# Differential attention on one core: scores in one two-bank tile, projections in three single banks, and three steps moved to VectorE

## The chip, the cores and the metric

The kernel runs on one core of a Trainium2 chip. The metric is the device time of one execution in microseconds. TensorE is called PE in the profile, VectorE DVE, ScalarE ACT, GpSimd POOL and SyncE SP.

## The reference, cut to what matters

The program is a two-layer diffusion block: 512 latent tokens and 256 context tokens of width 1024. Layer 0 is a feed-forward block, windowed attention and a second feed-forward block; layer 1 has a feed-forward block, differential attention, a feed-forward block and the last norm. The change is in differential attention alone. It has 8 heads; each has two pairs of queries and keys of 64 elements and one value of 128, and only the 512 latent tokens ask:

```python
def diff_probs(s):
    p = jax.nn.softmax(s * scale, axis=-1)          # scale = 64 ** -0.5 = 0.125
    return p[:, :, 0] - lam * p[:, :, 1]

def head_out(o):
    o = _rmsnorm(o, subln_w) * (1.0 - lambda_init)
    return o.reshape(o.shape[0], o.shape[1], H * 2 * HD) @ w_out

s_lat = jnp.einsum('bqhjd,bkhjd->bhjqk', qb, kx)
s_ctx = jnp.einsum('bqhjd,bchjd->bhjqc', qb, kc)
p = diff_probs(jnp.concatenate([s_lat, s_ctx], axis=-1))
```

All of it is in float32. The kernel splits each operand of a matmul into a rounded high part and the rest (names in `h` and `l`), and multiplies high by high, high by low and low by high; the scores hold the high and low part of the 64 key rows stacked as 128 rows, and so take two matmuls.

## The kernel before, in words

A tile scheduler sets the order of the instructions of each engine, from the program's order, the buffers of each pool and its own costs. Each engine then works its list in order.

`diff` (L586 on) opens four pools of PSUM, which has eight banks of 512 columns: `pss` with four banks for scores (tile name `s`), `ptr` with two for transposes (`tr`), `pav` with one for the head's output (`av`) and `pbig` with one for projections (`half`). The loop runs over heads `h` 0 to 7. In each head `probs` is called for four blocks of 128 queries (0 to 3, called q0 to q3 here); after q1, q2 and q3 the next head's keys, queries and values are projected (`keys`, `queries`, `vals`); last comes `values` for the head. In the last head the place of the projections is taken by `out_proj(0, ...)`, which multiplies heads 0 to 3 with the output weights, and behind the loop by `out_proj(1, ...)` for heads 4 to 7. The first three projections, for head 0, use the score banks.

A projection (`project_halves`, L265) takes 24 matmuls into one bank, then 24 into another; `scaled_halves` (L288, DVE) reads each bank out, times the tokens' norm. `rope` rotates keys and queries: a bias (L310, ACT), a shuffle (L313, DVE), times the cosine (L314, POOL), times the sine (L315, here on POOL), and the sum (L318, DVE). `vals` transposes the values (L661), rounds them (`vh`, L663, ACT) and takes the rest (`vl`, L664, DVE).

`probs` works for each of the two pairs j = 0, 1 in two chunks of 384 keys. For each chunk there are two matmuls into an own bank (L678, L679) and a maximum over the chunk (L680, DVE). L683 joins the two maxima, and ACT takes two exponentials with their sums (L686). Then the sums are added (L690), inverted (L691) and the second is multiplied by lambda (L692), all on DVE; POOL scales the second pair's 768 columns (L694) and DVE makes the difference (L695).

`values` takes six blocks of keys: four transposes (L703), a rounding (`pth`, L706, ACT), the rest (`ptl`, L707, DVE) and three matmuls into `av` (L708 to L710). Then the head's norm: squares (L715, ACT), a sum over partitions by a matmul with ones, in two passes (L717, PE, into a `tr` bank), three ACT steps (L718 to L720), four steps on POOL (L721 to L724), the product (L725, DVE), the output's high part (L727, ACT) and low part (L728, DVE).

Of the kernel before, what the change touches and what calls it, by code (L numbers as in the profile page):

```python
# [10 lines left out]
F32 = mybir.dt.float32  # L11
# [6 lines left out]
P = 128  # L18
# [16 lines left out]
class Net:  # L35
# [229 lines left out]
    def project_halves(self, src, xonly=False, pool=None, tag="half"):  # L265

        w = self.weights(src)
        pool = pool or self.pbig
        mm = self.nc.tensor.matmul
        cuts = ((CTX, 512), (512, T + 2)) if xonly else ((0, 384), (384, T + 2))  # L270
        out = []
        for s, e in cuts:
            ps = pool.tile([P, 512], F32, name=tag)
            for k in range(ND):
                for i, (w_, x) in enumerate(((w[0], self.xh), (w[0], self.xl), (w[1], self.xh))):
                    mm(ps[:, :e - s], w_[:, k], x[:, k, s:e], start=(k == 0 and i == 0), stop=(k == ND - 1 and i == 2))  # L276
            out.append(ps)
        n = 256 if xonly else 384
        bias = self.sp.tile([P, 2], F32, name="bias")
        self.nc.vector.tensor_copy(out=bias, in_=out[1][:, n:n + 2])  # L280
        return out, bias

    def scaled_halves(self, ps, tag, xonly=False):
        u = self.tp.tile([P, T], F32, name=tag)
        s, n = (CTX, 256) if xonly else (0, 384)
        for i in range(2):
            tk = slice(s + i * n, s + i * n + n)
            self.nc.vector.tensor_tensor(out=u[:, tk], in0=ps[i][:, :n], in1=self.rstd[:, tk], op=ALU.mult)  # L288
        return u
# [296 lines left out]
    def diff(self, after):  # L586
        nc, a = self.nc, self.a
        pss = self.ps("pdiff_s", 4)
        ptr = self.ps("pdiff_t", 2)
        pav = self.ps("pdiff_v", 1)  # L590
        self.pbig = self.ps("pdiff", 1)
# [20 lines left out]
        early = self.project_halves(a["diff_in"][8], pool=pss, tag="s")  # L612
        self.norm_halves(pss)
# [7 lines left out]
        def keys(h, early=None):  # L621
# [3 lines left out]
            self.rope(u, bias, u[:, XT], nc.gpsimd)  # L625
# [25 lines left out]
        def vals(h, pool=None):  # L651
            ps, bias = self.project_halves(a["diff_in"][16 + h], pool=pool, tag="s" if pool else "half")
# [15 lines left out]
        def probs(ks, qs, qb):  # L668
            st = self.sp.tile([P, 12], F32, name="st4")
            out = []  # L670
            qc = slice(qb * P, (qb + 1) * P)
            for j in range(2):
                p = (pp, p1p)[j].tile([P, T], F32, name=f"p{j}")
                ss = []
                for c in range(2):
                    s = pss.tile([P, 512], F32, name="s")[:, :384]
                    kc = ks[j][:, c * 384:(c + 1) * 384]
                    nc.tensor.matmul(s, qs[j][0][:, qc], kc, start=True, stop=False)  # L678
                    nc.tensor.matmul(s, qs[j][1][:, qc], kc, start=False, stop=True)  # L679
                    nc.vector.tensor_reduce(out=st[:, 2 * j + c:2 * j + c + 1], in_=s, op=ALU.max, axis=AX.X)  # L680
                    ss.append(s)
                nm = st[:, 4 + j:5 + j]
                nc.vector.tensor_scalar(out=nm, in0=st[:, 2 * j:2 * j + 1], scalar1=st[:, 2 * j + 1:2 * j + 2],  # L683
                                        scalar2=-0.125, op0=ALU.max, op1=ALU.mult)
                for c in range(2):
                    nc.scalar.activation(out=p[:, c * 384:(c + 1) * 384], in_=ss[c], func=AF.Exp, bias=nm, scale=0.125,  # L686
                                         accum_out=st[:, 6 + 2 * c + j:7 + 2 * c + j])
                out.append(p)
            r = self.sp.tile([P, 2], F32, name="rr")
            nc.vector.tensor_tensor(out=r, in0=st[:, 6:8], in1=st[:, 8:10], op=ALU.add)  # L690
            nc.vector.reciprocal(out=r, in_=r)  # L691
            nc.vector.tensor_tensor(out=r[:, 1:2], in0=r[:, 1:2], in1=lam[:, 2:3], op=ALU.mult)  # L692
            p0, p1 = out
            nc.gpsimd.tensor_scalar(out=p1, in0=p1, scalar1=r[:, 1:2], scalar2=1.0, op0=ALU.mult, op1=ALU.mult)  # L694
            nc.vector.scalar_tensor_tensor(out=p0, in0=p0, scalar=r[:, 0:1], in1=p1, op0=ALU.mult, op1=ALU.add)  # L695
            return p0

        def values(h, ps_, vh, vl):
# [22 lines left out]
            nc.gpsimd.tensor_tensor(out=v, in0=v, in1=r0, op=ALU.mult)  # L721
            nc.gpsimd.tensor_tensor(out=v, in0=v, in1=r0, op=ALU.mult)
            nc.gpsimd.tensor_scalar(out=v, in0=v, scalar1=-0.5, scalar2=1.5, op0=ALU.mult, op1=ALU.add)
            nc.gpsimd.tensor_tensor(out=r0, in0=v, in1=r0, op=ALU.mult)  # L724
# [29 lines left out]
        ks, qs, vv = keys(0, early), queries(0, pss), vals(0, pss)  # L754
# [21 lines left out]
        self.pbig.release(); pav.release(); ptr.release(); pss.release()  # L776
# [353 lines left out]
```

## Time and profile before

| | us |
|---|---|
| median of 3 runs | 2852.33 |
| lowest, highest | 2849.23, 2855.4 |
| profiled execution: its time | 2853.44 |
| profiled execution: its span | 2851.6 |

The mean granted clock of TensorE in the profiled execution is 0.991. The span is the time from the first to the last instruction in the trace, and starts at 0 there. Differential attention lies between 2065.7, where its first projection starts, and 2439.7, where the first matmul starts that needs the last head's output: 374.0 us. In the profile a line such as `L288` is a line of the kernel; `out<-in` are the program's tile names; behind `|` stand busy time, mean duration of one in ns, and the idle time of the engine ahead of it with what ended it. A row of the windows gives, behind its length, the busy time and count of PE, PEld (TensorE's weight loads), DVE, ACT and POOL, then the granted clock, the DMA share and GB/s.

### The profile page before, as it was taken

The numbers are of one execution on the slowest core, as the hardware profiler recorded it, in microseconds if no ns is written. First come the engines' busy times: TensorE is split into PE (matmuls) and PEld (weight loads), VectorE is DVE, ScalarE is ACT, GpSimd is POOL, SyncE is SP. The second block draws the span as 40 slices with busy tenths as digits, with TensorE's granted clock in tenths as the row PEclk, the third lists the DMA queues.
The fourth block names the chain that finished last, engine by engine and source line by source line (L and its number), as shares of the span: only waits on it lengthen the run. The fifth ranks groups of instructions, "written<-read, shape, count | busy, mean of one in ns | idle before, by whom it ended". The sixth has DMA issues, their size and how long they took to land. (4 is left out here: it accounts for less than half of the span.)

```text
span 2851.6 us, 40866 instructions
## 1 busy us (share of the span) xinstructions
PE 2759.4 (97%) x16162; PEld 2578.0 (90%) x16162; DVE 1525.4 (53%) x2661; ACT 962.6 (34%) x1733; POOL 1279.3 (45%) x756
## 2 busy tenths in 40 slices
PE   6999999999899999999999999999999999899998
PEld 4999999989777999999999999999988887799998
DVE  8645455567887844444557333333567777422223
ACT  3212112245666422121233221221345655422223
POOL 1434333365433533333444434333555665555553
PEclk9999999999999999999999999999999999999999
DMA  7332432342331223223323233233232233233331
GB/s 277 107 127 97 140 111 98 123 138 81 84 127 38 89 85 117 86 85 121 94 81 111 84 104 102 71 115 115 73 99 82 82 90 121 73 100 93 101 103 45
DMA packets 105119, 290.09 MB, mean 102 GB/s; under 512 B 12512, under 2 KB 22880, under 8 KB 104928
## 3 DMA queue, kind: packets, MB, share of 16 engines
q1 hardware_dynamic: 104496, 287.37, 31.3%
q8 instruction: 128, 2.10, 0.3%
q14 instruction: 63, 0.52, 0.1%
q10 hardware_dynamic: 432, 0.11, 0.0%
HBM read 257.28 MB, written 12.06 MB: 94 GB/s over the span
## 5 line engine op out<-in xcount | busy, mean ns | idle before, releaser
L56 POOL TENSOR_TENSOR w_lo<-w_raw,w_hi 128x1024 fp32r<-128x1024 f32 (+2 forms) x377 | 804.1, 2133 | 1089.8 <-ACT w_hi L55 1066.9
L55 ACT CAST w_hi<-w_raw 128x1024 fp32r<-128x1024 f32 (+2 forms) x377 | 337.5, 895 | 1112.4 <-PE big L70 398.2
L257 PE MATMUL big<-xh,w_hi 128*128 128x384 f32 (+3 forms) x2816 | 689.8, 326 | 6.5 <-DVE xh L174 3.2
L257 PE MATMUL big<-xh,w_lo 128*128 128x384 f32 (+3 forms) x2816 | 688.7, 326 | 0.6 <-POOL w_lo L56 0.5
L257 PE MATMUL big<-xl,w_hi 128*128 128x384 f32 (+3 forms) x2816 | 686.8, 325 | 0.9 <-DVE xl L185 0.9
L257 PEld LDWEIGHTS big<-xh,w_hi 128*128 128x128 f32 x2816 | 499.4, 190 | 10.0 <-DVE tb L210 3.7
L131 DVE SCALAR_TENSOR_TENSOR ada_junk<-w_raw,s_bc 128x1024 f32<-128x1024 f32 x224 | 337.4, 1506 | 305.9 <-DMA w_raw<-ada_w 303.7
L257 PEld LDWEIGHTS big<-xl,w_hi 128*128 128x128 f32 x2816 | 496.8, 190 | 1.1 <-DVE xl L185 1.1
L257 PEld LDWEIGHTS big<-xh,w_lo 128*128 128x128 f32 x2816 | 494.6, 189 | 1.6 <-POOL w_lo L56 1.6
L262 DVE COPY bias<-big 128x2 f32<-128x2 f32 x176 | 27.6, 157 | 597.0 <-PE big L257 596.9
L68 PE MATMUL big<-hh,w_hi 128*128 128x512 f32 (+1 forms) x1200 | 327.4, 344 | 0.0
L72 PE MATMUL big<-hh,w_lo 128*128 128x512 f32 (+1 forms) x1200 | 326.8, 344 | 0.0
L70 PE MATMUL big<-hl,w_hi 128*128 128x512 f32 (+1 forms) x1200 | 326.8, 343 | 0.0
L302 DVE SCALAR_TENSOR_TENSOR hT<-big,mod,hT 128x512 f32<-128x512 f32 (+1 forms) x288 | 167.9, 618 | 180.9 <-PE big L72 180.6
L70 PEld LDWEIGHTS big<-hl,w_hi 128*128 128x128 f32 x1200 | 225.6, 188 | 30.0
L72 PEld LDWEIGHTS big<-hh,w_lo 128*128 128x128 f32 x1200 | 224.7, 188 | 28.8
L68 PEld LDWEIGHTS big<-hh,w_hi 128*128 128x128 f32 x1200 | 224.8, 188 | 27.1
L991 POOL TENSOR_TENSOR hl<-tb,hh 128x768 fp32r<-128x768 f32 (+1 forms) x88 | 151.5, 1722 | 169.9 <-ACT hh L990 158.1
L986 DVE SCALAR_TENSOR_TENSOR tb<-tb,bias,ta 128x512 f32<-128x512 f32 (+1 forms) x154 | 179.6, 1199 | 8.3 <-DVE tb L295 0.5
L276 PE MATMUL half<-xh,w_hi 128*128 128x384 f32 (+3 forms) x464 | 155.4, 335 | 20.3 <-DVE ta L288 18.2
L990 ACT CAST hh<-tb 128x768 fp32r<-128x768 f32 (+1 forms) x88 | 68.7, 781 | 268.4 <-DVE tb L986 268.4
L276 PE MATMUL half<-xl,w_hi 128*128 128x384 f32 (+3 forms) x464 | 153.7, 331 | 0.0
(224 smaller groups left out, 3595.6 us busy)
## 6 DMA issues: line engine op xcount, KB each, us to landing
w_raw<-ffn_gu SPq DMA_DIRECT2D x176, 512.0 KB, 3.3
w_raw<-ada_w SPq DMA_DIRECT2D x128, 512.0 KB, 3.3
w_raw<-ffn_d SPq DMA_DIRECT2D x96, 256.0 KB, 2.7
w_raw<-ffn_d SPq DMA_DIRECT2D x64, 320.0 KB, 2.9
w_raw<-diff_in SPq DMA_DIRECT2D x24, 512.0 KB, 3.2
w_raw<-gqa_in SPq DMA_DIRECT2D x12, 512.0 KB, 3.5
ada_raw<-ada_w SPq DMA_DIRECT2D x8, 512.0 KB, 9.4
ada_rawk<-ada_k SPq DMA_DIRECT2D x8, 512.0 KB, 7.8
```

The lines of the kernel that those rows point to most:

```text
L55: nc.scalar.copy(out=hi[:, :cols], in_=raw[:, :cols])
L56: nc.gpsimd.tensor_tensor(out=lo[:, :cols], in0=raw[:, :cols], in1=hi[:, :cols].bitcast(F32), op=ALU.subtract)
L68: nc.tensor.matmul(o, wh, xh, start=(k == 0), stop=False)
L70: nc.tensor.matmul(o, wh, xl, start=False, stop=False)
L72: nc.tensor.matmul(o, wl, xh, start=False, stop=(k == n - 1))
L131: getattr(nc, engines[s]).scalar_tensor_tensor(out=junk, in0=raw, scalar=1.0, in1=self.sbc[:, s], op0=ALU.mult, op1=ALU.mult, accum_out=se ...
L257: mm(ps[:, c, :e - s], w[:, k], x[:, k, s:e], start=first, stop=last)
L276: mm(ps[:, :e - s], w_[:, k], x[:, k, s:e], start=(k == 0 and i == 0), stop=(k == ND - 1 and i == 2))
L302: self.nc.vector.scalar_tensor_tensor(out=h, in0=o, scalar=self.mv(l, s, c, d), in1=h, op0=ALU.mult, op1=ALU.add)
L986: nc.vector.scalar_tensor_tensor(out=u[:, tk], in0=u[:, tk], scalar=bu[:, s:s + 1], in1=g[:, tk], op0=ALU.add, op1=ALU.mult)
L990: nc.scalar.copy(out=hh[:, toks], in_=u[:, toks])
L991: nc.gpsimd.tensor_tensor(out=hl[:, toks], in0=u[:, toks], in1=hh[:, toks].bitcast(F32), op=ALU.subtract)
```

## The change

- **Banks.** The score pool holds one tile of two banks in place of four single banks, and the projections get three single banks in place of one.
- **Scores.** For each pair j the four matmuls go into the two banks of the one tile; one maximum (negated) runs over 768 columns, and one exponential with one sum. The factor 0.125 moves into the queries, where it is applied with the norm, so the joining step, the adding of the sums and the product with lambda go.
- **Second pair's scaling.** One DVE step with two scalars (the inverse and lambda) in place of the step on POOL.
- **Rope.** The product with the sine is on DVE in keys and queries.
- **Head norm.** Three DVE steps in place of four on POOL.
- **First projections.** Keys, queries and values of head 0 go through the projection banks; the norm over all tokens takes the score tile.

```diff
-        pss = self.ps("pdiff_s", 4)
+        pss = self.ps("pdiff_s", 1)
+        self.pbig = self.ps("pdiff", 3)
         ptr = self.ps("pdiff_t", 2)
         pav = self.ps("pdiff_v", 1)
-        self.pbig = self.ps("pdiff", 1)
...
-        early = self.project_halves(a["diff_in"][8], pool=pss, tag="s")
-        self.norm_halves(pss)
+        early = self.project_halves(a["diff_in"][8])
+        self.norm_banks(pss)
...
-            self.rope(u, bias, u[:, XT], nc.gpsimd)
+            self.rope(u, bias, u[:, XT])
...
             for j in range(2):
                 p = (pp, p1p)[j].tile([P, T], F32, name=f"p{j}")
-                ss = []
-                for c in range(2):
-                    s = pss.tile([P, 512], F32, name="s")[:, :384]
-                    kc = ks[j][:, c * 384:(c + 1) * 384]
-                    nc.tensor.matmul(s, qs[j][0][:, qc], kc, start=True, stop=False)
-                    nc.tensor.matmul(s, qs[j][1][:, qc], kc, start=False, stop=True)
-                    nc.vector.tensor_reduce(out=st[:, 2 * j + c:2 * j + c + 1], in_=s, op=ALU.max, axis=AX.X)
-                    ss.append(s)
-                nm = st[:, 4 + j:5 + j]
-                nc.vector.tensor_scalar(out=nm, in0=st[:, 2 * j:2 * j + 1], scalar1=st[:, 2 * j + 1:2 * j + 2],
-                                        scalar2=-0.125, op0=ALU.max, op1=ALU.mult)
-                for c in range(2):
-                    nc.scalar.activation(out=p[:, c * 384:(c + 1) * 384], in_=ss[c], func=AF.Exp, bias=nm, scale=0.125,
-                                         accum_out=st[:, 6 + 2 * c + j:7 + 2 * c + j])
+                s = pss.tile([P, 2, 512], F32, name="s")[:, :, :384]
+                for i in range(2):
+                    for c in range(2):
+                        nc.tensor.matmul(s[:, c], qs[j][i][:, qc], ks[j][:, c * 384:(c + 1) * 384], start=(i == 0),
+                                         stop=(i == 1))
+                nc.vector.tensor_reduce(out=nm[:, j:j + 1], in_=s, op=ALU.max, axis=AX.XY, negate=True)
+                nc.scalar.activation(out=p.rearrange("p (c n) -> p c n", c=2), in_=s, func=AF.Exp, bias=nm[:, j:j + 1],
+                                     accum_out=sm[:, j:j + 1])
                 out.append(p)
-            r = self.sp.tile([P, 2], F32, name="rr")
-            nc.vector.tensor_tensor(out=r, in0=st[:, 6:8], in1=st[:, 8:10], op=ALU.add)
-            nc.vector.reciprocal(out=r, in_=r)
-            nc.vector.tensor_tensor(out=r[:, 1:2], in0=r[:, 1:2], in1=lam[:, 2:3], op=ALU.mult)
+            nc.vector.reciprocal(out=r, in_=sm)
             p0, p1 = out
-            nc.gpsimd.tensor_scalar(out=p1, in0=p1, scalar1=r[:, 1:2], scalar2=1.0, op0=ALU.mult, op1=ALU.mult)
+            nc.vector.tensor_scalar(out=p1, in0=p1, scalar1=r[:, 1:2], scalar2=lam[:, 2:3], op0=ALU.mult, op1=ALU.mult)
             nc.vector.scalar_tensor_tensor(out=p0, in0=p0, scalar=r[:, 0:1], in1=p1, op0=ALU.mult, op1=ALU.add)
...
-            nc.gpsimd.tensor_tensor(out=v, in0=v, in1=r0, op=ALU.mult)
-            nc.gpsimd.tensor_tensor(out=v, in0=v, in1=r0, op=ALU.mult)
-            nc.gpsimd.tensor_scalar(out=v, in0=v, scalar1=-0.5, scalar2=1.5, op0=ALU.mult, op1=ALU.add)
-            nc.gpsimd.tensor_tensor(out=r0, in0=v, in1=r0, op=ALU.mult)
+            nc.vector.tensor_tensor(out=v, in0=v, in1=r0, op=ALU.mult)
+            nc.vector.scalar_tensor_tensor(out=v, in0=v, scalar=-0.5, in1=r0, op0=ALU.mult, op1=ALU.mult)
+            nc.vector.scalar_tensor_tensor(out=r0, in0=v, scalar=1.5, in1=r0, op0=ALU.add, op1=ALU.mult)
             nc.vector.tensor_tensor(out=r0, in0=r0, in1=flat(av), op=ALU.mult)
...
-        ks, qs, vv = keys(0, early), queries(0, pss), vals(0, pss)
+        ks, qs, vv = keys(0, early), queries(0), vals(0)
```

The scheduler puts the work in a new order. In the rows below each line is a line of that kernel, a name's number is its buffer, and `x2` stands for two such instructions in a row. "Group" means the four score matmuls of one query block and one pair j.

**TensorE in the last two heads.** Before, in head 7, the second pair of q2 and the first pair of q3: each has two buffers, and a row stands for one score matmul. `half` with `w_hi` is the output projection of heads 0 to 3, twelve matmuls of which follow on the last row.

```order
L678 MATMUL s_21412<-ks_20980,qh_21087 128x384
L679 MATMUL s_21412<-ks_20980,ql_21088 128x384
L678 MATMUL s_21416<-ks_20980,qh_21087 128x384
L679 MATMUL s_21416<-ks_20980,ql_21088 128x384
L710 MATMUL av_21205<-ptl_21260,vh_20745 128x512
L678 MATMUL s_21465<-ks_20979,qh_21085 128x384
L679 MATMUL s_21465<-ks_20979,ql_21086 128x384
L678 MATMUL s_21469<-ks_20979,qh_21085 128x384
L679 MATMUL s_21469<-ks_20979,ql_21086 128x384
L746 MATMUL half_21436<-xl_8633,w_hi_21430 128x512
```

Now, in head 6 (q2 and the first group of q3): `tr<-acc` is the sum for the norm of head 5, `tr<-ident,ta` the transposes of head 7's values, `tr<-ident,p0` those of this head's probabilities.

```order
L708 MATMUL s_20695<-ks_20285,qh_20380 128x384 x2
L708 MATMUL s_20695<-ks_20285,ql_20381 128x384 x2
L739 MATMUL tr_20563<-acc_91,ones_80 128x512
L690 MATMUL tr_20878<-ident_75,ta_20871 128x128 x3
L690 MATMUL tr_20884<-ident_75,ta_20871 128x128 x3
L708 MATMUL s_20703<-ks_20286,qh_20382 128x384 x2
L708 MATMUL s_20703<-ks_20286,ql_20383 128x384 x2
L725 MATMUL tr_20891<-ident_75,p0_20578 128x128
L725 MATMUL tr_20891<-ident_75,p0_20598 128x128
L708 MATMUL s_20795<-ks_20285,qh_20380 128x384 x2
L708 MATMUL s_20795<-ks_20285,ql_20381 128x384 x2
```

All 96 matmuls of the output projection of heads 0 to 3 now stand ahead of this, in heads 5 and 6; from the second group of head 6's q1 on, thirteen groups have no projection between them.

**TensorE in the middle heads.** Before, in head 4, q0: all eight score matmuls of the query block, both pairs of it in four buffers, stood between the transposes of the values (`tr<-ident,ta`) and the next projection.

```order
L661 MATMUL tr_19861<-ident_75,ta_19848 128x128 x3
L678 MATMUL s_19958<-ks_19641,qh_19747 128x384
L678 MATMUL s_19962<-ks_19641,qh_19747 128x384
L678 MATMUL s_19970<-ks_19642,qh_19749 128x384
L678 MATMUL s_19974<-ks_19642,qh_19749 128x384
L679 MATMUL s_19970<-ks_19642,ql_19750 128x384
L679 MATMUL s_19974<-ks_19642,ql_19750 128x384
L679 MATMUL s_19958<-ks_19641,ql_19748 128x384
L679 MATMUL s_19962<-ks_19641,ql_19748 128x384
L276 MATMUL half_20049<-xh_8632,w_hi_20019 128x386
```

Now, in head 4 (the same in heads 2 and 3), at the first group of q2: the first transposes of the probabilities stand behind those of the values, in the same two `tr` banks.

```order
L739 MATMUL tr_19761<-acc_91,ones_80 128x512
L690 MATMUL tr_20076<-ident_75,ta_20069 128x128 x3
L708 MATMUL s_19893<-ks_19483,qh_19578 128x384 x2
L708 MATMUL s_19893<-ks_19483,ql_19579 128x384 x2
L690 MATMUL tr_20082<-ident_75,ta_20069 128x128 x3
L725 MATMUL tr_20089<-ident_75,p0_19776 128x128
```

A little further on, at q3 of the same head, its two groups have two transposes between them.

```order
L708 MATMUL s_19993<-ks_19483,qh_19578 128x384 x2
L708 MATMUL s_19993<-ks_19483,ql_19579 128x384 x2
L725 MATMUL tr_20089<-ident_75,p0_19892 128x128
L725 MATMUL tr_20101<-ident_75,p0_19892 128x128
L708 MATMUL s_20001<-ks_19484,qh_19580 128x384 x2
L708 MATMUL s_20001<-ks_19484,ql_19581 128x384 x2
```

The two pairs of a query block, which stood side by side, now stand apart, each group in the one tile `s`. Counted by the spacing of matmuls that the prediction reads from the trace, TensorE has 4.5 us of work in this head from the start of q2's first group to the start of its second, 6.0 us from there to q3's first, and 0.9 us from there to q3's second.

**VectorE in the same head.** Before, at q0: the maxima of the query block stand together, behind the values' low parts and the norm's product.

```order
L664 TENSOR_TENSOR vl_19854<-tr_19855,vh_19853 128x384
L725 TENSOR_TENSOR hT_7787<-hT_7787,av_19421 128x2x256
L664 TENSOR_TENSOR vl_19854<-tr_19861,vh_19853 128x384
L680 TENSOR_REDUCE st4_19956<-s_19970 128x1
L680 TENSOR_REDUCE st4_19956<-s_19974 128x1
L680 TENSOR_REDUCE st4_19956<-s_19958 128x1
L680 TENSOR_REDUCE st4_19956<-s_19962 128x1
```

Now, in head 4, between the two maxima of q2 stand the values' low parts (the first is left out here), the next queries' read-out and rope, and the norm of head 3 (`hT`).

```order
L311 SCALAR_TENSOR_TENSOR ta_20370<-half_20318,rstd_90 128x256
L311 SCALAR_TENSOR_TENSOR ta_20370<-half_20343,rstd_90 128x256
L743 TENSOR_TENSOR hT_7787<-hT_7787 128x2x256
L693 TENSOR_TENSOR vl_20075<-tr_20082,vh_20074 128x384
L744 SCALAR_TENSOR_TENSOR hT_7787<-hT_7787 128x2x256
L339 STREAM_SHUFFLE tb_20374<-ta_20370 128x512
L745 SCALAR_TENSOR_TENSOR hT_7787<-hT_7787 128x2x256
L341 TENSOR_TENSOR tb_20374<-tb_20374,sin_85 128x512
L746 TENSOR_TENSOR hT_7787<-hT_7787,av_19687 128x2x256
L344 TENSOR_TENSOR ta_20370<-sq_20375,tb_20374 128x512
L710 TENSOR_REDUCE st4_19891<-s_19901 128x1
```

The maximum at the end of these rows is that of the second group.

More of the change, by code (lines that the diff above doesn't have):

```diff
@@ L263, in projected, with project_banks, bias_of, norm_banks @@
         return ps[:, :, :n], bias
-    def project_halves(self, src, xonly=False, pool=None, tag="half"):
+    def project_banks(self, src, pool, xonly=False, scale=None):
+        ps = pool.tile([P, 2, 512], F32, name="s")
+        self.project_k([(self.weights(src), ps)], range(ND), xonly)
+        n = 256 if xonly else 384
+        return (ps[:, 0], ps[:, 1]), self.bias_of(ps[:, 1, n:n + 2], scale)
+    def bias_of(self, ps, scale=None):
+        bias = self.sp.tile([P, 2], F32, name="bias")
+        if scale:
+            self.nc.vector.tensor_scalar(out=bias, in0=ps, scalar1=scale, scalar2=None, op0=ALU.mult)
+        else:
+            self.nc.vector.tensor_copy(out=bias, in_=ps)
+        return bias
+    def norm_banks(self, pool):
+        ps = pool.tile([P, 2, 512], F32, name="s")
+        for i in range(2):
+            tk = slice(i * 384, i * 384 + 384)
+            self.nc.tensor.matmul(ps[:, i, :384], self.ones, self.acc[:, tk], start=True, stop=True)
+        for i in range(2):
+            tk = slice(i * 384, i * 384 + 384)
+            self.rsqrt(self.rstd[:, tk], ps[:, i, :384], 1.0 / D)
+    def project_halves(self, src, xonly=False, pool=None, tag="half", scale=None):
         w = self.weights(src)
@@ L278, in project_halves, with scaled_halves @@
         n = 256 if xonly else 384
[L279 to L283, printed above, removed]
+        return out, self.bias_of(out[1][:, n:n + 2], scale)
+    def scaled_halves(self, ps, tag, xonly=False, scale=None):
         u = self.tp.tile([P, T], F32, name=tag)
@@ L287, in scaled_halves @@
             tk = slice(s + i * n, s + i * n + n)
-            self.nc.vector.tensor_tensor(out=u[:, tk], in0=ps[i][:, :n], in1=self.rstd[:, tk], op=ALU.mult)
+            if scale:
+                self.nc.vector.scalar_tensor_tensor(out=u[:, tk], in0=ps[i][:, :n], scalar=scale, in1=self.rstd[:, tk],
+                                                    op0=ALU.mult, op1=ALU.mult)
+            else:
+                self.nc.vector.tensor_tensor(out=u[:, tk], in0=ps[i][:, :n], in1=self.rstd[:, tk], op=ALU.mult)
         return u
```

16 lines of the change are left out of this document (10 added, 6 removed).

## Prediction, made before the changed kernel ran

> **What bounds the kernel now.** I read the busy times of the engines first, then the windows of differential attention, cut at four events of TensorE, then the waits inside it.
>
> ```profile
> PE 2759.4 (97%) x16162; PEld 2578.0 (90%) x16162; DVE 1525.4 (53%) x2661; ACT 962.6 (34%) x1733; POOL 1279.3 (45%) x756
> ```
>
> The windows run from the first projection to the norm of head 0, from there to that of head 5, and from there to the first matmul that needs the last head:
>
> ```profile
> 2065.70:2167.40 101.70, 93.02 (x554) 87.37 (x553) 74.51 (x149) 50.36 (x112) 58.66 (x37) 0.98 0.32 92
> 2167.40:2364.10 196.70, 184.69 (x1109) 171.73 (x1108) 147.78 (x318) 114.23 (x269) 121.14 (x81) 0.99 0.29 84
> 2364.10:2439.70 75.60, 63.64 (x287) 49.65 (x285) 43.10 (x81) 33.58 (x74) 36.15 (x25) 0.95 0.35 113
> ```
>
> The stage takes 374.0 us and TensorE is busy 341.3 of them; VectorE has 265.4, ScalarE 198.2, GpSimd 215.9. TensorE bounds it, and a gain can only come from the 32.7 it idles or from its clock. The waits that end last on it:
>
> ```profile
> PE half L276 <- DVE ta L288: 17.4, 14, 2.1
> ...
> PE o L746 <- ACT o L727: 3.9, 1, 3.9
> ...
> PE half L747 <- DMA xl<-od: 2.8, 1, 2.8
> ```
>
> The first is the single projection bank: the second half's matmuls wait until VectorE has read the first half out. What TensorE must do at the least I take from the spacing of matmuls in the timeline:
>
> ```profile
> 2092.62 0.34 PE L276 MATMUL half<-xh,w_hi 128*128 128x384 f32 x1
> 2092.80 0.34 PE L276 MATMUL half<-xl,w_hi 128*128 128x384 f32 x1
> 2092.97 0.34 PE L276 MATMUL half<-xh,w_lo 128*128 128x384 f32 x1
> ...
> 2149.89 0.60 PE L703 MATMUL tr<-ident,p 128*128 128x128 f32 x4
> 2150.25 0.37 PE L276 MATMUL half<-xh,w_lo 128*128 128x258 f32 x1
> ...
> 2364.12 1.02 PE L717 MATMUL tr<-acc,ones 128*128 128x512 f32 x2
> ```
>
> A 384-column matmul takes 0.175, by proportion 0.12 at 256 and 0.23 at 512; a transpose takes 0.09 (four in 0.36), the norm's sum 1.0. One head has 96 projection matmuls of 384 and 48 of 256 columns, 32 for scores, 30 transposes, 18 of 512 and a sum: 16.8 + 5.8 + 5.6 + 2.7 + 4.1 + 1.0 = 36.0. Eight heads give 288; 96 matmuls of the output projection of heads 0 to 3 22, 36 of the next one 8.3, the first norm 1.5: some 320. So 54 of the 374 are lost: the waits above 17.4 + 3.9 + 2.8; other idle time 8.6; the clock (0.02 x 101.7 + 0.01 x 196.7 + 0.05 x 75.6) 7.8; and 13 where matmuls change their shape.
>
> **The change part by part.** The matmuls stay, so the 320 stay. Removed or shortened are:
>
> ```profile
> L686 ACT ACTIVATE p<-s,st 128x384 f32<-128x384 f32 x128 | 73.2, 584 | 43.2 <-DVE st L683 43.2
> L680 DVE TENSOR_REDUCE st<-s 128x1 f32<-128x384 f32 x128 | 66.3, 548 | 10.6 <-PE s L679 10.4
> ...
> L695 DVE SCALAR_TENSOR_TENSOR p<-p,rr,p 128x768 f32<-128x768 f32 x32 | 51.6, 1619 | 7.2 <-POOL p L694 7.2
> ...
> L694 POOL TENSOR_SCALAR p<-p,rr 128x768 f32<-128x768 f32 x32 | 31.1, 971 | 58.4 <-DVE rr L692 52.3 <-ACT oh L727 1.8 <-DVE bias L280 1.6
> ...
> L686 ACT ACTIVATION_READ_ACCUMULATOR p<-s,st 128x1 f32 x128 | 26.2, 205 | 0.0
> ...
> L315 POOL TENSOR_TENSOR tb<-tb,sin 128x512 f32<-128x512 f32 x16 | 21.6, 1353 | 2.7 <-DVE tb L313 1.9 <-DVE rr L692 0.8
> ...
> L690 DVE TENSOR_TENSOR rr<-st 128x2 f32<-128x2 f32 x32 | 17.1, 536 | 9.9 <-ACT p L686 9.9
> ...
> L692 DVE TENSOR_TENSOR rr<-rr,lam 128x1 f32<-128x1 f32 x32 | 13.0, 406 | 0.7
> ...
> L683 DVE TENSOR_SCALAR st<-st 128x1 f32<-128x1 f32 x64 | 12.4, 202 | 0.1
> ...
> L664 DVE TENSOR_TENSOR vl<-tr,vh 128x384 fp32r<-128x384 f32 x16 | 8.6, 551 | 5.7 <-ACT vh L663 5.6
> ...
> L691 DVE RECIPROCAL rr<-rr 128x2 f32<-128x2 f32 x32 | 5.0, 156 | 0.4
> ```
>
> (L664, L691 and L695 stay.) The new forms stand nowhere in the trace; their nearest rows, from the other attentions, from rope and from the read-out of queries, are:
>
> ```profile
> L441 ACT ACTIVATE p<-s,st 128x512 f32<-128x512 f32 x32 | 21.9, 689 | 11.3 <-PE tr L466 7.2 <-DVE st L438 3.4 <-PE s L429 0.7
> L434 DVE TENSOR_REDUCE st<-s 128x1 f32<-128x512 f32 x32 | 21.6, 684 | 7.0 <-PE s L432 6.9
> ...
> L313 DVE STREAM_SHUFFLE tb<-ta 128x512 f32<-128x512 f32 x26 | 19.3, 740 | 0.0
> ...
> L315 DVE TENSOR_TENSOR tb<-tb,sin 128x512 f32<-128x512 f32 x10 | 10.1, 1006 | 0.2
> ...
> L288 DVE TENSOR_TENSOR ta<-half,rstd 128x256 f32<-128x256 f32 x14 | 5.8, 411 | 0.7 <-PE half L276 0.7
> ...
> L451 DVE TENSOR_SCALAR p<-p,st 128x640 f32<-128x640 f32 x8 | 5.1, 632 | 0.1
> ...
> L213 DVE SCALAR_TENSOR_TENSOR tb<-tb,ta 128x768 f32<-128x768 f32 x3 | 2.9, 956 | 0.1
> ```
>
> The maximum goes from 548 to 684 ns over 128 more columns, so 768 take 0.955 (bounds 0.68 and 2 x 0.548). The exponential, 584 to 689, gives 0.90 (0.69 to 1.17). The scale takes 0.76 by proportion (0.63 to 0.97). Of the head norm, the last steps before were:
>
> ```profile
> 2433.43 1.28 POOL L721 TENSOR_TENSOR hT<-hT 128x512 f32<-128x512 f32 x1 [8.23 <-ACT hT L720]
> ...
> 2438.17 0.69 DVE L725 TENSOR_TENSOR hT<-hT,av 128x512 f32<-128x512 f32 x1 [9.04 <-POOL hT L724]
> 2438.89 0.72 ACT L727 ACTIVATE o<-hT,subw 128x512 fp32r<-128x512 f32 x1 [5.54 <-DVE hT L725]
> ```
>
> GpSimd's four steps take 4.7 from end to end; three on VectorE take 3 x 0.69 = 2.1.
>
> VectorE: 66.3 + 12.4 + 17.1 + 13.0 = 109 go; 64 x 0.955 + 32 x 0.76 + 16 x 1.0 + 24 x 0.69 = 118 come, so it stands at 274 of 374 and can keep up on average. ScalarE loses 29, GpSimd 31 + 22 + 38; neither bounds anything, and their relief costs and gains nothing but by what follows.
>
> Gained on the path: the waits for the read-out, 17.4, and the half clock behind them, about 3 (two drops of 1.5, below). With three banks, a projection's second half has one at once, and the next has its first half read out during 24 matmuls, 4 us against VectorE's 0.5; if VectorE is up to 3 us late that cover still holds. The last norm gains 2.6 of the 3.9 that TensorE waited at L746.
>
> Lost on the path: one score tile serves all groups. A group's four matmuls take 3 x 0.175 + 0.34 = 0.87, its maximum 0.955, its exponential 0.90; with three hand-overs of 0.05 (from L725's end at 2438.86 to L727's start it was 0.03) and half the 0.205 of the accumulator's read, since I can't tell which of the two frees the tile, the next group may start 3.0 after this one started. Where other work of TensorE fills these 3.0, it costs nothing; I walked through the order.
>
> - Heads 2, 3 and 4. Between the starts of q3's groups lies 0.9 of work: wait 2.1. At q2 the transposes of q0 need a `tr` bank that is freed by `vl` (0.55), which stands behind the maximum; TensorE gets there at 1.24 after the values' transposes start, VectorE at 0.27 + 0.87 + 0.955 + 0.55 = 2.6: wait 1.3. Between q2's maxima VectorE has 2 x 0.55 + 2 x 0.41 + 0.74 + 1.0 + 5 steps of 0.69 = 7.1; the second one ends 0.87 + 0.955 + 7.1 + 0.955 = 9.9 after q2's start, the tile is free at 11.0, and TensorE is there at 4.5 + 6.0 = 10.5: wait 0.5. Together 3.9, three heads 11.7; for heads 1 and 5, where only some of these places recur, 4: **15.7**.
> - The end. From head 6's q1 on, thirteen groups follow without a projection, with 19.3 of work from the first's start to the last's: twelve steps of 3.0 are 36, the least. Where a block is finished, VectorE puts reciprocal, scale and difference (0.16 + 0.76 + 0.96 to 1.62) ahead of the next group's maximum, which was ready 0.87 after the tile was freed: 1.0 to 1.7 more in every second step, so 3.5 to 3.85 a step. I take 3.6, that is 43, a loss of **24**. These groups had the output projection among them before.
> - The last block. Maximum to difference is 4.4 with eleven matmuls (2.5) as cover: 1.9 lost, and 1.3 left of the last norm's wait: **3**.
>
> The sum: 320 + 4 (the first projection's start) + 2.8 (DMA) + 9 for changes of shape and 2 for the clock (13 and 7.8 - 3, without the share of the tail, which is priced whole) + 15.7 + 24 + 3 = 380.7, that is 6.7 above 374.0. The profiled execution took 2853.44, 1.1 above the median of 2852.33: 2860.1 there, **2859** against the median. The other idle time, 4.6 beside the start, goes up in the new waits.
>
> [...]
>
> **The clock.** Two stretches of 4 us in which TensorE was idle for 1.85 and 1.65, each with the 4 us that follow:
>
> ```profile
> 2200.00:2204.00 4.00, 2.15 (x10) 1.67 (x9) 3.17 (x7) 1.58 (x6) 2.78 (x3) 0.94 0.28 105
> 2204.00:2208.00 4.00, 4.00 (x16) 4.00 (x16) 0.85 (x1) 0.58 (x1) 1.35 (x1) 0.63 0.48 111
> ...
> 2284.00:2288.00 4.00, 2.35 (x11) 1.53 (x10) 2.43 (x9) 3.22 (x10) 2.93 (x3) 1.00 0.23 94
> 2288.00:2292.00 4.00, 3.35 (x19) 3.03 (x18) 3.82 (x4) 1.61 (x3) 4.00 (x3) 1.00 0.39 90
> ```
>
> After one the granted clock fell to 0.63, which costs 0.37 x 4 = 1.5; after the other it stayed at 1.00. In the tail each wait is about 2 with work of 1.6 between. I count no loss there, since at half clock that work takes 3.2 and still fits in the step of 3.6 but for the group's own 0.87.
>
> **The rivals.**
>
> 1. *Faster: the single tile turns round faster.* If VectorE keeps the maxima ahead (step 3.0) and only q3's wait is left in the middle heads (8 in all), 7.2 + 7.7 less are lost: 365.8, or **2844**. For it: VectorE idles 29% of the stage. Against it: its order puts the block's finish ahead of the maximum. It decides below 3.5 us a step with the middle at 8. Chance 0.22.
> 2. *The clock drops in the tail and behind the middle waits.* A group's 0.87 then takes 0.7 more, 13 times 9, and three times 1.5 in the middle: 13 more, **2872**. For it the 0.63, against it the 1.00. [...] Chance 0.14.
> 3. *The change doesn't do what it says: half of the read-out waits stay*, because VectorE, with 7.1 of work in one run, reads the banks out too late for three to do: 8.7 more, **2868**. Against it: 4 us of cover for each bank. Chance 0.12.
>
> My forecast keeps 0.52, its own range from the tail's 3.3 and 4.1 a step and the bounds of maximum and exponential: 2850 to 2868. The whole range, 2844 to 2875, takes in the rivals' points. 0.2% is 5.7 us, about what a measurement of this kernel can tell from no change. Slower by more is two thirds of the forecast case and rivals 2 and 3 (0.34 + 0.26, less 0.06 for their low ends): 0.54. Faster is most of rival 1 and little else: 0.19. The same is the rest: 0.27.
>
> **What would show it.** PE's wait for the read-out (half from DVE ta) should be gone or under 3 us; a wait of PE for the score tile from ACT's exponential should appear, 2 us at q3 of heads 2 to 4 and about 2 per group in some 43 us before the last out projection; the first matmul on the last head's output should wait 1.3. The maximum should take 0.955, the exponential 0.90, the scale 0.76. I am wrong if the groups of the tail start 3.0 apart or under, if read-out waits of over 5 us remain, or if the windows of the tail show a clock under 0.9.

## The result, and the profile after

The changed kernel takes 2887.58 us (median of 4 runs, 2885.18 to 2892.06) against 2853.86 for the kernel before in the same measurement: ratio 1.0122, 95% interval 1.0102 to 1.0141, 34 us slower. The forecast was 2859 with a range of 2844 to 2875: the sign was right, but the loss forecast was a fifth of the one measured. The profiled execution took 2886.53 with a span of 2884.7.

The page of the changed kernel shows TensorE 13 us busier with the same 16162 matmuls, GpSimd 89 us less busy:

```profile
PE 2772.3 (96%) x16162; PEld 2585.7 (90%) x16162; DVE 1538.4 (53%) x2541; ACT 950.2 (33%) x1605; POOL 1190.4 (41%) x676
```

The windows of differential attention, cut at the same events (first projection, norm matmuls of heads 0 and 5, first matmul on the last head's output; busy time and count of PE, PEld, DVE, ACT and POOL, then granted clock, DMA share, GB/s):

```profile
2067.34:2178.90 111.56, 108.06 (x663) 104.30 (x663) 74.61 (x113) 48.16 (x79) 52.42 (x27) 0.98 0.34 99
2178.90:2403.30 224.40, 200.18 (x1108) 179.90 (x1107) 165.17 (x252) 110.08 (x195) 72.39 (x36) 0.97 0.31 92
2403.30:2470.31 67.01, 45.29 (x169) 31.52 (x168) 40.61 (x60) 26.78 (x52) 0.00 (x0) 0.77 0.12 41
```

The stage takes 403.0 in place of 374.0. Its last part holds 118 TensorE instructions fewer than before and is only 8.6 shorter: that is the run of groups without other work, at a granted clock of 0.77. The first part holds 109 more, since with three banks the projections run ahead. The waits of TensorE in the stage and behind it:

```profile
PE s L708 <- ACT p L711: 14.3, 11, 2.1
PE tr L725 <- DVE p L717: 6.7, 6, 2.3
PE tr L725 <- DVE vl L693: 5.9, 5, 1.3
PE half L300 <- DVE ta L314: 4.9, 2, 2.7
PE tr L739 <- ACT acc L737: 4.1, 6, 0.7
PE o L767 <- DMA o<-od: 2.8, 1, 2.8
PE o L767 <- DVE hT L746: 2.7, 1, 2.7
```

The read-out wait fell from 17.4 to 4.9, as forecast in kind; the first three lines hardly stood there before (0.4 for the score buffers, none for the others), and the clock is lower. The groups whose price the forecast gave:

```profile
L710 DVE TENSOR_REDUCE st<-s 128x1 f32<-128x768 f32 x64 | 61.0, 953 | 23.1 <-PE s L708 22.8
L711 ACT ACTIVATE p<-s,st 128x768 f32<-128x768 f32 x64 | 57.7, 901 | 68.7 <-DVE st L710 68.1
...
L717 DVE SCALAR_TENSOR_TENSOR p<-p,st,p 128x768 f32<-128x768 f32 x32 | 32.8, 1026 | 0.7
L716 DVE TENSOR_SCALAR p<-p,st,lam 128x768 f32<-128x768 f32 x32 | 32.5, 1015 | 1.1
...
L744 DVE SCALAR_TENSOR_TENSOR hT<-hT 128x512 f32<-128x512 f32 x8 | 10.8, 1348 | 0.1
```

Maximum and exponential came as worked out (0.955 and 0.90). The scaling took 1.015 where I took 0.76; the difference behind it came down from 1.619 to 1.026, so a block's finish (0.16 + 1.015 + 1.026) cost 2.2, inside the 1.9 to 2.5 that I had. The second step of the head norm (L744), which I priced at 0.69, took 1.35 in the mean of the eight heads, and 0.69 in the last.

One bare step in the timeline, in head 7, from a group's first matmuls to those of the next:

```profile
2438.56 0.62 PE L708 MATMUL s<-ks,qh 128*128 128x384 f32 x2 [1.46 <-ACT p L711]
...
2439.57 0.96 DVE L710 TENSOR_REDUCE st<-s 128x1 f32<-128x768 f32 x1
...
2440.56 0.90 ACT L711 ACTIVATE p<-s,st 128x768 f32<-128x768 f32 x1 [2.05 <-DVE st L710]
2441.36 0.19 ACT L711 ACTIVATION_READ_ACCUMULATOR p<-s,st 128x1 f32 x1
...
2441.60 1.01 PE L708 MATMUL s<-ks,qh 128*128 128x384 f32 x2 [2.08 <-ACT p L711]
```

From start to start it is 3.04. The next group starts 0.05 behind the accumulator's read. The first two matmuls of the second group take 1.01 where those of the first took 0.62: the granted clock in the trace goes from 1.00 to 0.50 at 2440.36.

For the accounts below I took, for every matmul of the timeline, the time from its start to the next one's start and split it: its spacing at full clock (0.175 at 384 columns and so on), the wait that the timeline shows ahead of the next, what the halved clock added, and a rest. The account runs from the first projection to the first matmul of the feed-forward block behind the attention, so that it does not depend on what is done last. Changes of shape are in the rest: from start to start the first 384-column matmul behind a transpose took 0.26 for 0.175 (median of 26 in the trace before and of 23 in the changed one), the first of 512 columns 0.315 for 0.23 (13 in the trace before).

| kernel | median us | stage | work | waits | halved clock | rest |
|---|---|---|---|---|---|---|
| before | 2852 to 2855 | 390.9 | 329.9 | 32.2 | 8.5 | 20.3 |
| changed | 2887.6 | 422.1 | 330.7 | 50.2 | 18.5 | 22.8 |
| two_tiles | 2840.4 | 375.2 | 330.2 | 24.7 | 3.1 | 17.3 |
| moves_only | 2860.6 | 396.7 | 330.9 | 37.7 | 8.5 | 19.6 |
| moves_undone | 2899.1 | 435.6 | 330.4 | 59.5 | 24.3 | 21.5 |
| one_proj_bank | 2897.3 | 432.4 | 330.6 | 59.0 | 18.5 | 24.2 |
| two_proj_banks | 2887.1 | 420.2 | 331.1 | 49.5 | 18.4 | 21.3 |
| warm | 2886.9 | 418.2 | 344.0 | 39.9 | 11.0 | 23.4 |
| warm_8 | 2888.9 | 423.1 | 338.0 | 45.2 | 17.1 | 22.8 |
| two_tiles_pool | 2849.3 | 385.5 | 330.9 | 30.5 | 9.5 | 14.5 |
| two_two_one | 2899.1 | 436.2 | 330.9 | 50.4 | 28.7 | 26.2 |
| late_fill | 2885.2 | 419.5 | 331.0 | 49.7 | 15.8 | 23.0 |
| three_tr_banks | 2903.8 | 437.2 | 331.3 | 57.3 | 30.7 | 18.0 |

From before to changed the stage grew by 31.2: 18.0 of waits, 10.0 of halved clock, 2.5 of rest, and 0.8 of work. Both stretches hold the same 2004 matmuls, so the 0.8 is an error of the split. The split says where TensorE's time went in one trace; it does not say what would be left without the halved clock.

### The profile page after: what moved, and what is told of

Same layout as the page of the kernel before. It is cut to its first block, busy times and chain, and to the rows that moved or that the text cites. A ratio compares the mean times of both kernels' runs of the same rounds, so it can differ in the third digit from the quotient of the medians.

```text
span 2884.7 us, 40537 instructions
## 1 busy us (share of the span) xinstructions
PE 2772.3 (96%) x16162; PEld 2585.7 (90%) x16162; DVE 1538.4 (53%) x2541; ACT 950.2 (33%) x1605; POOL 1190.4 (41%) x676
## 4 chain that ended last, share of the span: by engine, by line
PE 63%; DVE 5%; ACT 2%; POOL 1%; issue 1%; DMA 1%; SPq 0%; DVEq 0%; POOLq 0%; ACTq 0%
PE big L257 34%; PE big L68 5%; PE big L72 5%; PE big L70 5%; PE half L300 5%; PE half L552 2%; PE s L708 1%; DVE st L710 1%; ACT p L711 1%; POOL w_lo L56 1%; PE tr L725 1%; DVE p L716 0%; PE tr L492 0%; PE av L732 0%; PE av L730 0%
## 5 line engine op out<-in xcount | busy, mean ns | idle before, releaser
L300 PE MATMUL half<-xh,w_hi 128*128 128x386 f32 (+3 forms) x512 | 172.1, 337 | 7.8 <-DVE ta L314 5.7
L300 PE MATMUL half<-xh,w_lo 128*128 128x386 f32 (+3 forms) x512 | 170.3, 333 | 0.5 <-POOL w_lo L56 0.5
L300 PE MATMUL half<-xl,w_hi 128*128 128x386 f32 (+3 forms) x512 | 170.5, 333 | 0.0
```

## The experiments

My theory after the result: the single score tile makes each group wait for its own maximum and exponential, and this, with the clock that falls behind such waits, costs some 46 us, of which the projection banks give 13 back. The rivals: the steps moved to VectorE stand ahead of the maxima and are the cost; or the order is, which runs projections and the output projection ahead and leaves the tail bare.

**Two tiles (two_tiles).** One line gives the scores a second tile, and the projections pay with two banks:

```diff
-        pss = self.ps("pdiff_s", 1)
-        self.pbig = self.ps("pdiff", 3)
+        pss = self.ps("pdiff_s", 2)
+        self.pbig = self.ps("pdiff", 1)
-        early = self.project_halves(a["diff_in"][8])
+        early = self.project_banks(a["diff_in"][8], pss)
-        ks, qs, vv = keys(0, early), queries(0), vals(0)
+        ks, qs, vv = keys(0, early), queries(0, pss), vals(0, pss)
```

> Two score tiles of two banks, one projection bank as before, first projections of head 0 through the score tiles; every other part of the change stays. Theory (the single tile's turnaround, 3.0 us and more a group, with the clock falling behind its waits, costs some 46 us, of which 13 come back at the projections): TensorE's waits for the score tile fall from 14.3 us to under 3, the output projection of heads 0 to 3 stands between the last groups again, the read-out waits come back to 10 to 18, and the time is 2840 to 2857. Rival (the steps moved to VectorE are what costs, since they stand ahead of the maxima): it stays above 2870.

Measured: 2840.43 us against 2852.9, ratio 0.9958 (0.9941 to 0.9975), faster than both kernels. Its waits of TensorE in the stage:

```profile
PE half L300 <- DVE ta L311: 6.9, 6, 1.2
PE half L300 <- DVE ta L314: 6.7, 7, 2.7
PE s L708 <- DMA ql<-ql: 3.6, 6, 2.1
PE s L257 <- DVE tb L210: 3.4, 1, 3.4
PE o L767 <- DVE hT L746: 2.7, 1, 2.7
```

The wait for the score tile is gone, the read-out waits are back at 13.6, and the end (from head 5's norm on) is dense:

```profile
2358.57:2430.00 71.43, 65.51 (x311) 53.54 (x311) 42.74 (x65) 30.71 (x52) 16.30 (x8) 0.98 0.37 122
```

The rival that blames the moves is out as the main cause: all of them are in this kernel.

**The moves alone (moves_only).** The kernel before, with its four score banks, and scaling, sine product and head norm on VectorE:

```diff
-            nc.gpsimd.tensor_scalar(out=p1, in0=p1, scalar1=r[:, 1:2], scalar2=1.0, op0=ALU.mult, op1=ALU.mult)
+            nc.vector.tensor_scalar(out=p1, in0=p1, scalar1=r[:, 1:2], scalar2=1.0, op0=ALU.mult, op1=ALU.mult)
-            self.rope(u, bias, u[:, XT], nc.gpsimd)
+            self.rope(u, bias, u[:, XT])
-            nc.gpsimd.tensor_tensor(out=v, in0=v, in1=r0, op=ALU.mult)
...
+            nc.vector.scalar_tensor_tensor(out=r0, in0=v, scalar=1.5, in1=r0, op0=ALU.add, op1=ALU.mult)
```

> The kernel before with nothing but the three moves to VectorE: the second pair's scaling, the product with the sine, the head norm (here the four steps without the sum and lambda joined for the scaling, three steps for the norm). Theory: 2846 to 2860, no change clear of noise, VectorE busy some 320 us of the stage. Rival (moves cost): slower by 12 or more.

Measured: 2860.64 against 2852.9, ratio 1.0026 (1.0016 to 1.0037): 7.7 slower, which neither side had as its number. VectorE is then busy 305 of the 377 us around the stage, 266 before; first row before, second this one:

```profile
2067.00:2444.00 377.00, 345.09 (x1952) 311.99 (x1953) 266.06 (x547) 197.90 (x454) 214.65 (x142) 0.98 0.31 91
```

```profile
2067.00:2444.00 377.00, 341.07 (x1939) 310.75 (x1939) 305.05 (x615) 198.64 (x453) 128.20 (x64) 0.97 0.31 93
```

and the read-out comes later, 22.7 for 17.4, with one wait of 4.0 (before, the longest was 2.1):

```profile
PE half L276 <- DVE ta L288: 22.7, 13, 4.0
```

**The moves undone (moves_undone).** The changed kernel with the same steps back on GpSimd; the scaling, for one:

```diff
-            nc.vector.tensor_scalar(out=p1, in0=p1, scalar1=r[:, 1:2], scalar2=lam[:, 2:3], op0=ALU.mult, op1=ALU.mult)
+            nc.vector.tensor_tensor(out=r[:, 1:2], in0=r[:, 1:2], in1=lam[:, 2:3], op=ALU.mult)
+            nc.gpsimd.tensor_scalar(out=p1, in0=p1, scalar1=r[:, 1:2], scalar2=1.0, op0=ALU.mult, op1=ALU.mult)
```

> The changed kernel with scaling, sine product and head norm back on GpSimd; the one score tile and the three projection banks stay. Theory: still slow, 2872 to 2892, with 14 us or more of waits for the tile and the clock halved for 20 us or more of the last 65. Rival (moves cost): below 2862.

Measured: 2899.13, ratio 1.0161 (1.0146 to 1.0177), 7 above what I expected and 11.6 above the changed kernel. With one tile the moves help: the difference (L718 here) waits for GpSimd's scaling, and the next maxima stand behind it. The first matmul on the last head's output waits 5.2 here, 2.7 in the changed kernel.

```profile
L718 DVE SCALAR_TENSOR_TENSOR p<-p,st,p 128x768 f32<-128x768 f32 x32 | 47.4, 1481 | 11.3 <-POOL p L717 11.3
```

**Two tiles without the moves (two_tiles_pool).** The edits of two_tiles and of moves_undone together; what is left of the change is the arithmetic of the scores:

```diff
-        pss = self.ps("pdiff_s", 1)
+        pss = self.ps("pdiff_s", 2)
...
-            self.rope(u, bias, u[:, XT])
+            self.rope(u, bias, u[:, XT], nc.gpsimd)
```

> Two score tiles and one projection bank, with scaling, sine product and head norm back on GpSimd. What is left of the change is the arithmetic of the scores alone (one maximum, one exponential, 0.125 in the queries). With one score tile the moves were worth 11.6 us, in the kernel before they cost 7.7. If their gain is that they shorten the chain behind the tile, two tiles take it away: 2836 to 2848, within 6 us of two_tiles. If the moves help with this arithmetic in any case: 2848 to 2858.

Measured: 2849.32 against 2855.25, ratio 0.9977 (0.9967 to 0.9987). That is just inside the second answer and 9 above two_tiles; but the kernel before was 2.4 slower in this measurement than in that of two_tiles, and with each counted against its own the distance is 6.5 (5.9 and 12.5 faster than before), with intervals of the two ratios that meet. So the second answer is likelier, and not shown. The four corners, counted in this way: in the old arithmetic the moves cost 7.7; in the new one they gain 12.5 with one score tile and about 6.5 with two. The new arithmetic by itself takes VectorE from 266 to 243 of 377 us, and the moves bring it to 281; on the old arithmetic they bring it to 305. First row without, second with the moves:

```profile
2067.00:2444.00 377.00, 346.52 (x1971) 317.46 (x1970) 242.96 (x392) 190.94 (x333) 215.38 (x145) 0.97 0.31 91
```

```profile
2067.00:2444.00 377.00, 351.82 (x2016) 319.24 (x2015) 280.88 (x440) 196.34 (x340) 137.71 (x69) 0.99 0.32 94
```

The 377 us hold more of the stage in a faster kernel. Over the whole stage, up to the feed-forward block, VectorE is busy 281 before, 321 with the moves alone, 252 with the new arithmetic and 282 with both: the order is the same. That this load is why the moves cost in one case and gain in the other is argued from these sums; no run shows it.

**One projection bank (one_proj_bank).** One score tile, one projection bank, four transposition banks; the norm over all tokens uses two of the latter.

```diff
-        self.pbig = self.ps("pdiff", 3)
-        ptr = self.ps("pdiff_t", 2)
+        self.pbig = self.ps("pdiff", 1)
+        ptr = self.ps("pdiff_t", 4)
-        early = self.project_halves(a["diff_in"][8])
+        early = self.project_banks(a["diff_in"][8], pss)
```

> The changed kernel with one projection bank and four transposition banks: one score tile as in the change, but the output projection of heads 0 to 3 can't run ahead into heads 5 and 6 and stands between groups of head 7. If the loss is the tail without work between groups, six or more of the thirteen bare steps are covered: the read-out waits come back (some 15 us) and the tail gives 15 to 20, so 2875 to 2890. If the single tile costs wherever it stands, and the fill in the tail is of no use, the read-out waits add up: 2895 to 2910.

Measured: 2897.25, ratio 1.0156 (1.0141 to 1.0171): the upper answer. Six of the twelve bare steps had projections between their groups now, as the theory asked, without the 15 to 20 that it promised. The read-out took 15.0 more (13.6 in the loop and 6.3 at the first projections, against 4.9), the other waits together 6.2 less, and the halved clock stayed at 18.5. Beside two_tiles this is the closest comparison on the score tile: both have one projection bank and the moves, and with one score tile and two more transposition banks in place of the second tile the kernel is 57 us slower.

**Two projection banks, and idle transposes (two_proj_banks, warm, warm_8).** The control has two projection banks. The others put idle transposes into the bank set free, behind each group of the tail (warm_8 with 8 in place of 12):

```diff
-        self.pbig = self.ps("pdiff", 3)
+        self.pbig = self.ps("pdiff", 2)
...
+                src = out[0] if j else last[0]
+                for t in range(n):
+                    nc.tensor.transpose(warm[:, t % 4 * P:(t % 4 + 1) * P], src[:, t % 6 * P:(t % 6 + 1) * P], self.ident)
...
-                ps_.append(probs(ks, qs, i))
+                ps_.append(probs(ks, qs, i, 12 if h == 7 or h == 6 and i > 1 else 0))
```

> The changed kernel with two projection banks in place of three; one bank stays unused. It is the control for the next run. Expected 2880 to 2895 by both theories: the tail has its bare groups as with three banks.

> The same, and the unused bank takes twelve idle transposes (1.07 us of TensorE's time, their results not used) behind the matmuls of each group in head 6 from q2 on and in head 7, where TensorE waits for the score tile. Theory (the halved clock is a cost of its own, some 10 us in the last 65): the granted clock of the tail stays over 0.95 and the time falls by 6 to 12 against two_proj_banks, though TensorE does 13 us more work. Rival (the wait alone costs, the clock only shows it): no gain, 0 to 10 us more.

> As warm, with eight idle transposes (0.71 us) behind a group and none behind the last one, which in warm stood on the path. Against two_proj_banks (2887): if the halved clock is a cost of its own, the tail keeps the clock over 0.9, and 4 to 10 us are gained: 2877 to 2883. If not, 2884 to 2892.

Measured: 2887.05, 2886.85 and 2888.93 (ratios 1.0108, 1.0106 and 1.0121; intervals some 0.0016 either way). The third bank is worth nothing. The idle transposes did hold the clock; the tail of the control, then of warm:

```profile
2402.60:2450.00 47.40, 29.46 (x107) 19.75 (x105) 32.72 (x48) 21.09 (x40) 3.00 (x1) 0.70 0.10 34
```

```profile
2408.14:2455.80 47.66, 36.70 (x233) 32.23 (x233) 32.50 (x47) 20.35 (x40) 2.18 (x1) 0.93 0.14 48
```

The halved clock's share fell from 18.4 to 11.0 and the waits from 49.5 to 39.9, but 13 us of transposes did not all fall into waits: some stood on the path (one batch waited 2.4 for the difference that it reads, with a group queued behind it), so nothing was gained: the rival's number. With eight the clock was not held (17.1), and the time was again that of the answer without a gain. That the clock can be bought back this way is not shown, and neither that it can't: what came back was spent on the transposes.

**Another fill for the tail (late_fill).** The output projection inside the loop takes heads 2 to 5, so it can't start ahead of head 5's output:

```diff
-                        nc.sync.dma_start(first[r][c].bitcast(F32), od[r, c])
+                        nc.sync.dma_start(first[r][c].bitcast(F32), od[(2, 3, 4, 5)[r], c])
-        for h in range(4, 7):
+        for h in (0, 1, 6):
```

> The changed kernel with the halves of the output projection dealt out anew: the first half, which runs inside the head loop, takes heads 2 to 5 in place of 0 to 3, and the last one heads 0, 1, 6 and 7 (the weights' rows are laid out accordingly). So these 96 matmuls can't run ahead of head 5's output and stand between the groups of head 7; about six bare steps are left in head 6. Theory (bare steps of the single tile are the cost, wherever the order puts them; cover takes them away): seven steps with 22 us of work among them save their waits and the halved clock, 8 to 18 us: 2869 to 2880. Rival (the tile's turnaround costs the same with work between): 2883 to 2892.

Measured: 2885.18, ratio 1.0115 (1.01 to 1.013): the rival's answer. In the timeline head 7's first groups had their cover, and bare steps of 3.2 to 5.2 stood in head 6 and at the end instead. The fill was only moved, so the theory's condition, more cover, was not met; what the run shows is that this other order gained nothing.

**Three transposition banks (three_tr_banks).** So that the transposes of the probabilities need not wait for the values' low part:

```diff
-        self.pbig = self.ps("pdiff", 3)
-        ptr = self.ps("pdiff_t", 2)
+        self.pbig = self.ps("pdiff", 2)
+        ptr = self.ps("pdiff_t", 3)
```

> The changed kernel with two projection banks and three transposition banks. If the wait of the transposes for the bank that the values' low part holds (some 1.3 us in five heads, and a halved clock behind some of them) is a cost of its own, it goes: 5 to 10 us, 2877 to 2882. If TensorE only waits later for the next score tile in its place: 2883 to 2890.

Measured: 2903.78, ratio 1.0174 (1.0159 to 1.0189): 16.7 slower than the control, outside both answers. The wait for `vl` did fall (5.9 in the changed kernel, 1.5 in the control, 1.0 here), but the waits for the score tile rose from 18.8 to 21.7, those for the difference from 2.4 to 11.5, and the halved clock from 18.4 to 30.7:

```profile
PE s L708 <- ACT p L711: 21.7, 12, 3.4
PE tr L725 <- DVE p L717: 11.5, 8, 3.6
```

The scheduler had made another order with the new bank; why that order is so much worse I did not settle.

**Two, two and one (two_two_one).** On top of two_tiles, a second projection bank in place of one for the transposes:

```diff
-        self.pbig = self.ps("pdiff", 1)
-        ptr = self.ps("pdiff_t", 2)
+        self.pbig = self.ps("pdiff", 2)
+        ptr = self.ps("pdiff_t", 1)
```

> Two score tiles, two projection banks and one transposition bank, the moves as in the change. Theory: TensorE needs turnaround cover at every place; the read-out waits fall under 5 us (gain 9 to 12 against two_tiles), but the single transposition bank, read by ScalarE and then VectorE in each of 48 rounds of values, gives 0.5 to 1.4 us of wait where no other work stands between: 5 to 40 us lost. I expect 2845 to 2875, slower than two_tiles. Rival (the projections' banks are what matters): 2825 to 2838.

Measured: 2899.13, ratio 1.0149 (1.0134 to 1.0164), slower still than expected, and outside both answers. The read-out waits fell to 6.1, not under 5. The single transposition bank is now what TensorE waits for:

```profile
PE av L730 <- ACT pth L728: 14.9, 21, 1.1
PE s L708 <- ACT p L711: 6.7, 11, 1.1
```

## Why the prediction was wrong

What held: the places and the chain. The waits for the score tile and for the values' low part are those that the forecast named, a bare step's least is 3.04 for 3.0, the twelve steps of the tail (2399.29 to 2446.00) took 46.7, or 3.9 each, for 43 and 3.6; maximum and exponential came to the hundredth. And two_tiles shows that the single tile is what costs: with the second one 47 us go, though two projection banks are given up for it.

What failed is the step that put the halved clock at next to nothing, and with it the sum, 380.7 for the stage (its terms as printed give 380.5) where it took 403.0. One of the prediction's own signs of being wrong says the same: a clock under 0.9 in the windows of the tail; it was 0.77. The 22.3 between sum and measurement:

- **The clock, 14.9.** "I count no loss there, since at half clock that work takes 3.2 and still fits in the step of 3.6 but for the group's own 0.87." The account has 16.9 of halved clock in the stage where the sum had 2: 7 in the tail, the rest in five drops ahead of it and one behind it. Eight windows at the tail's start, 3.41 us each:

```profile
2402.77:2406.19 3.42, 2.39 (x12) 1.32 (x10) 2.42 (x3) 2.20 (x4) 0.00 (x0) 1.00 0.19 75
2406.19:2409.60 3.41, 1.45 (x7) 0.85 (x6) 2.58 (x5) 2.60 (x7) 0.00 (x0) 1.00 0.02 5
2409.60:2413.01 3.41, 2.08 (x6) 1.58 (x6) 3.41 (x8) 0.72 (x1) 0.00 (x0) 0.51 0.00 0
2413.01:2416.43 3.42, 1.97 (x6) 1.46 (x6) 2.02 (x3) 0.99 (x2) 0.00 (x0) 0.50 0.37 137
2416.43:2419.84 3.41, 1.65 (x4) 1.14 (x4) 2.28 (x5) 0.99 (x2) 0.00 (x0) 0.50 0.05 17
2419.84:2423.25 3.41, 2.81 (x7) 1.98 (x8) 2.24 (x4) 1.97 (x4) 0.00 (x0) 0.50 0.00 0
2423.25:2426.67 3.42, 3.42 (x14) 3.04 (x13) 1.53 (x2) 0.59 (x1) 0.00 (x0) 0.50 0.00 0
2426.67:2430.08 3.41, 3.35 (x18) 2.62 (x17) 2.31 (x6) 1.97 (x4) 0.00 (x0) 1.00 0.00 0
```

  Once halved the clock stays so through five windows, until one is busy from end to end. I had priced a drop as 4 us behind one wait. The trace before held a longer one that the prediction did not look at; behind a window with 1.01 of matmuls the clock stays halved for two:

```profile
2370.77:2374.18 3.41, 1.01 (x5) 0.41 (x3) 1.57 (x5) 2.07 (x3) 3.33 (x3) 1.00 0.90 281
2374.18:2377.59 3.41, 2.26 (x7) 1.88 (x8) 0.00 (x0) 0.00 (x0) 3.33 (x3) 0.50 0.66 178
2377.59:2381.01 3.42, 3.42 (x13) 3.23 (x12) 2.43 (x5) 0.96 (x2) 0.34 (x1) 0.50 0.95 287
```

  Work that piles up in such a stretch is not hidden in the wait: the step at 2418.01 holds 2.4 of work and takes 6.1. In the middle a drop came in four of the five intervals between the norms of heads 0 and 5, 1.5 each.
- **The middle heads, 5.8.** I priced q3, the transposes and the late maximum in three heads, and 4 for heads 1 and 5. All five intervals show 4.7 to 5.1 of waits, 24.2 together, of which 2.7 is read-out: 21.5 for 15.7. The places were right: 2.5 at q3 for 2.1, in the three heads forecast, and 0.9 to 1.3 for `vl`, but in five heads. Missing were the waits of 0.7 for the norm's squares and 0.3 for the values' transposes in nearly every head, and 2.7 at the output projection's matmuls in the last interval; 1.7 of that is a transfer that the sum had priced apart, with 2.8.
- **The read-out, 4.9.** That "a projection's second half has one at once" held but for two waits of 2.7 and 2.2.
- **The tail's steps, -3.3**, without the clock's 7 that lie in them: 39.7 for 43.

These make the 22.3; the last block's waits (6.2 for 3, with the 2.8 for the transfer of `o` among them) and the smaller terms cancel. Taken by kinds, the stage's waits add up to 49.4, and the sum had 49.5 (4 + 2.8 + 15.7 + 24 + 3, where the tail's 24 holds its changes of shape too): the waits that came out longer are made up by those at the start and in the tail, which came out shorter. So the clock is the one large term that the sum lacked. Outside the stage come 4.1: it starts 1.6 later, and behind it are 9 output matmuls more than before (36 stood ahead of the last head's output, now 27), 2.1 of the 2.5.

How much of the 14.9 would come back as waits at full clock stays open: in the tail 3.3 of its 7 fell into room that the forecast had, and the idle transposes of warm, which held the clock, took up what they gave back.

Rival 2 was this mechanism, and its price of 13 is near the 14.9; I gave it 0.14. That the two agree so well is in part luck: it had 9 in the tail for 7, and 4.5 in the middle for the 9.9 outside the tail. What spoke against it, the window whose clock stayed at 1.00 behind 1.65 of idle time, was one case; the tail repeats such a wait at nearly every step, and the two drops there lasted 17.1 and 13.7 us, where the drop at 2203.5 in the trace before, the one that the prediction read as 0.63, lasted 3.41. The range ended at that rival with nothing else added, so the middle heads, the read-out and the 4.1 outside the stage (14.8 together) lay beyond it.

## What to carry to other kernels

A buffer that is read out by a chain of two engines wants a second one, unless the filler between its uses is longer than the chain at every place, not on average: here 330 us of work over 64 groups are 5.2 a group, against a chain of 3.04, and late_fill only moved the bare places. Price a run of waits on TensorE twice, once as idle time and once as the halved clock that can follow it: here the waits grew by 18.0 us, the halved clock by 10.0, and the longest drop lasted five windows of 3.41 us, until one was busy from end to end. And judge a move from one engine to another in the kernel that it will stand in: the same three moves cost 7.7 us in one arithmetic and gained 12.5 in the other with one score tile.

## What the runs showed of the hardware

- **In the traces before and changed the granted clock read 1.00 or 0.50, and it came back behind fuller windows than those behind which it fell.** Around differential attention (2050 to 2520) each change of it lay on the edge of a window of 3.41 us, as in the rows above. It fell four times in the kernel before and eight times in the changed one, each time behind a window in which PE was busy for 3 to 54% of the time; of the windows with 52 to 54% some were followed by a fall and some not, and none with more was. Eight of the drops lasted 3.41, two 6.83, one 13.65 and one 17.07. Each of the twelve ended behind a window that PE filled from end to end; behind halved windows filled to 18 to 83% it stayed at 0.50.
- **The accumulator's read seems to belong to the chain.** In the bare step the exponential ends at 2441.46 and the read of its sum at 2441.55; the next group starts at 2441.60, a hand-over of 0.05 from the read, as from the maximum to the exponential (2440.53 to 2440.56) it is 0.03.
- **The same step of VectorE took different times in different kernels.** The difference over 768 columns took 1.03 in the changed kernel, 1.20 in two_tiles, 1.29 in moves_only, and 1.48 to 1.62 where GpSimd does the scaling; the scaling itself 0.72 in two_tiles and 1.015 in the changed kernel. GpSimd's scaling beside it goes with the longest times of the difference; that it causes them, and what lies behind the rest, was not tested.
